# Delta rule: the 16x16 diagonal blocks of a triangular inverse on GpSimd instead of TensorE

## The chip, the cores and the metric

One core of one Trainium2 chip runs the whole kernel as one program. The metric is the device time of one execution in microseconds (us); the median of several runs counts. TensorE does the matrix products, VectorE, ScalarE and GpSimd the elementwise work, and SyncE, ScalarE and GpSimd issue the transfers (DMAs). In the rows of the profile they stand as PE (PEld is its weight load), DVE, ACT, POOL and SP.

## The reference, cut to what matters

One inference step of a decoder of two layers, for a prompt of 256 tokens and 8 samples of one token, width 2048. A layer mixes (four mLSTM heads and eight heads of the gated delta rule, from one input projection), attends to a memory of 256 tokens, and runs a SwiGLU feed-forward. The part that the change touches is the delta rule over the prompt:

```python
def step(S, xs):                                  # one chunk of the prompt
    qc, kc, vc, gc, bc = xs
    g = jnp.cumsum(gc, axis=1)
    ...
    kk = jnp.einsum('bthd,bshd->btsh', kc, kc)
    A = jnp.where(strict[None, :, :, None], decay_ts * kk * bc[:, None, :, :], 0.0)
    eg = jnp.exp(g)
    rhs = vc - eg[..., None] * jnp.einsum('bthd,bhde->bthe', kc, S)
    U = lax.linalg.triangular_solve(jnp.transpose(A, (0, 3, 1, 2)), jnp.transpose(rhs, (0, 2, 1, 3)),
                                    left_side=True, lower=True, unit_diagonal=True)
    wu = bc[..., None] * jnp.transpose(U, (0, 2, 1, 3))
    ...
```

For each head and chunk a unit triangular system (I + A) U = rhs is solved. The reference cuts the prompt into chunks of 64 tokens; the kernel takes two chunks of 128 and computes the same recurrence.

## The kernel before, in words

**Streams.** All large products are weight streams. A block of 128 x 1024 weights (512 KB) is loaded by SyncE into one of four buffers `raw`, and split exactly into two parts of float32r: `wh` by ScalarE (a copy that rounds) and `wl` by VectorE (`raw - wh`), three buffers each. TensorE then runs 24 products of 264 columns (256 tokens and 8 samples) on a block, into `acc`. Loads and splits carry a higher priority than the rest.

**Order of TensorE.** Its order is written by hand, by a small planner. A chain of small products is a generator that yields how long its next product must wait for other engines, in ns (`yield 2100.0`). `clock` adds up TensorE's own work as it is issued, by a formula (columns / 2.4 ns, four times that for float32); `pump()`, called after every few products of a stream, issues the next piece of each chain whose time on this clock has come. The planner fixes an order alone: if an input is late on the chip, TensorE waits. The order of the other engines, SyncE's queue and GpSimd's among them, comes from the scheduler's simulation, by priority and readiness; they keep that order too.

**The mixers.** Per layer, four groups of two delta-rule heads. For each group three streams (`q`, `k`, `v`) are followed by a convolution on VectorE (`y`, with a small part of it on GpSimd) and an activation (`s`). Then two chains start: `gdn_prompt` for the 256 tokens and `gdn_sample` for the samples (its products `dks` and `dS`; GpSimd makes `wm` for the latter). A group's `gdn_prompt` starts only after that of the group before has `formed` its states. GpSimd also loads states (`S`, `Ct`) and takes roots and reciprocals as powers (`kd`, `qd`, `oss`).

**gdn_prompt.** Four matrices at a time (two heads, two chunks), 128 x 128 each, side by side in tiles of 128 x 512. In order: keys transposed (`kT`); the products `kk` and `kq`; `N`, strictly upper triangular, by four VectorE operations (line 57); values and queries transposed (`vT`, `qT`). Then the inverse `Dm` of I + N and its transpose `Dt`. `Dm` starts as `ident`; a block size of 1 is doubled on VectorE alone (`u`). `N` is transposed by TensorE (`NT`) and copied to `A` by ScalarE. For b = 2, 4, 8, 16, 32, 64 a doubling step follows: four products `pp` (from `A` and `Dm`), a masked copy `Pf` on VectorE, four products `pd` (from `Dt` and `Pf`), `Dm` less `pd` on VectorE, and up to b = 16 a transposition of `Dm` to `Dt` on VectorE. Each half step is a yield (2100 ns ahead of `pp`, 1900 ns ahead of `pd`). A product in float32 shows as two matmul records in the trace. After the inverse come the two chunks (`pu`, `pS`, `pr`), and after a hold of 14200 ns the transposition `oT` of the output.

Small helpers record most operations, so that many rows carry their lines: L72 is `mm`, L76 `tr` (TensorE), L60 `tt`, L57 `stt` (VectorE, `tt` also GpSimd), L54 `copy` (ScalarE), L245 the load of `raw`, L807 and L734 the stores of delta-rule states.

Of the kernel before, what the change touches and what calls it, by code (L numbers as in the profile page):

```python
# [8 lines left out]
F32 = mybir.dt.float32  # L9
F32R = mybir.dt.float32r  # L10
AF = mybir.ActivationFunctionType
ALU = mybir.AluOpType
# [3 lines left out]
P = 128  # L16
D = 2048
KT = D // P
T = 256
# [11 lines left out]
PRIO = 1000  # L31
Q0, K0, V0, O0 = 0, 512, 1024, 2048
# [6 lines left out]
def bc(ap, axis, n):  # L39
    """ap with a new dimension of n at axis, of step 0."""  # L40
    a = ap.unsqueeze(axis)
    shape = list(a.shape)
    shape[axis] = n
    return a.to_broadcast(shape)
# [3 lines left out]
def kernel(ctx: ExitStack, tc: tile.TileContext, io: dict, outs: list):  # L48
# [14 lines left out]
    # A chain is a generator: it yields how long its next product must wait for other engines (ns). The clock counts  # L63
    # the tensor engine's work as it is issued; it only sets the order.
# [43 lines left out]
    pm = ctx.enter_context(tc.tile_pool(name="misc", bufs=4, space=PSUM))  # L108

# [10 lines left out]
    # exponents  # L120
# [4 lines left out]
    def power(t, e):  # L125
        """t ** e for e = hp, hm, in place"""
        if len(t.shape) == 3:
            e = e[:t.shape[0], :t.shape[1] * t.shape[2]].rearrange("p (a b) -> p a b", a=t.shape[1])
        else:
            e = e[:t.shape[0], :t.shape[1]]  # L130
        tt(t, t, e, ALU.pow, pool)

    # shf: out[m] = in[m - 32] - in[m] for m >= 32, on 64 partitions
# [6 lines left out]
    # for block size b: up[p, j] = 1 where row p is in the first half of pair j of blocks  # L140
    up = {}
    b = 1
# [10 lines left out]
    # twos[p, r] = 1 at p = 64 + r and 96 + r for r < 8, and at p = r - 8 and 24 + r for the others  # L153
# [4 lines left out]
    # msk[p, b] = 1 where p % 32 == b; hsel[p, h] = 1 where p % 4 == h  # L158
# [33 lines left out]
    def consts():  # L192
# [3 lines left out]
        # the gains of heads stand before 1 + tanh, twice the sigmoid  # L196
# [37 lines left out]
    def split_gain(h, l, src, g):  # L234
        """the parts of src * g, g per partition"""
        copy(h, src, scale=g)
        stt(l, src, g, h.bitcast(F32), ALU.mult, ALU.subtract)
# [11 lines left out]
    def stream(src, r0, nk, f0, xs, n=2):  # L249
        """[128, C] sums over nk row tiles, for n = 2 or 4 tiles of columns from f0; xs(k) gives the two parts of x."""  # L250
# [16 lines left out]
    def add_stream(src, r0, nk, hh, hl, nx=None, n=2):  # L267
        """x += src[r0 : r0 + nk * 128]^T h; the last one hands each tile to the next norm"""
# [10 lines left out]
    class Norm:  # L279
# [36 lines left out]
        def turn(self, t0):  # L316
            """tiles from t0, time on partitions"""
# [25 lines left out]
    def scaled(o, nx, out, k=1.0):  # L343
        """out[:, j] = k * r * o[j]"""
# [33 lines left out]
    class Gates:  # L378
        """tq: see there; over the samples: gs, exp(log decay) | a on all partitions; gn, exp(log decay), beta | a, w,
        exp(-m) with the samples on partitions; over the prompt, time on partitions: gT with m at 0, c at 32, sums of  # L380
        log decay at 64, beta at 96; em = exp(-m); eg and en = +-exp(sum of log decay) in the second chunk"""

    def gates(l, o, nx, mx, G, rstd):
# [8 lines left out]
        with tc.high_priority(offset=PRIO):  # L392
# [7 lines left out]
            # ln(1 + e) = ln(u) + (e - (u - 1)) / u with u = 1 + e as it rounds  # L400
# [7 lines left out]
            # log forget gate, its sums over time  # L408
# [11 lines left out]
            # log decay of the delta rule, its sums over each chunk  # L420
# [9 lines left out]
            # beta  # L430
# [4 lines left out]
            # c = i - b, M = max(m0, running max of c), m = b + M  # L435
        yield 20000.0
        with tc.high_priority(offset=PRIO):
# [15 lines left out]
            # the rows to spread over all partitions, in two parts: log decay sums at 64 and 96, M at 32 and 0  # L453
# [43 lines left out]
    def spread(out, G, r):  # L497
        """row r of tq's sums of parts on every partition: log decay sums of head r, or M of head r - 8"""
        mm(out, bc(twos[:, r], 1, P), G.tq)

# [1 line left out]
    def three(dst, src, swap):  # L502
        """the parts of src on 8 partitions at rows 0, 32 and 64: h, h, l, or with swap h, l, h"""
# [5 lines left out]
    def rank1(S, k3, r3, decay, mx, w):  # L509
        """S[b] = decay[b] * S[b] + k[b] r[b]^T, for states [128, 8, w]"""  # L510
# [11 lines left out]
    # Products of the samples' queries with their matrix memories, in float32r: block b of kqz, 40 b + 32 on, holds the  # L522
    # parts of sample b's query at b and 64 + b. Blocks overlap; rows that other samples' columns reach are not read.
    def columns(kqz, j, src):
        """the two parts of src, [128, 8]"""
# [4 lines left out]
    def state_parts(S, M):  # L530
        """the two parts of states, [128, 512]"""
# [5 lines left out]
    class Mix:  # L537
        """tiles of the mixers' pool"""
# [9 lines left out]
        def n(self, name, shape=(2, P)):  # L548
            """samples on partitions"""
# [24 lines left out]
    def gdn_decay(g, G, M, R):  # L574
        """E[s, i, t] = exp(sum of log decays over (s, t]), 0 for t < s; eL = exp(sum over the second chunk)"""
# [16 lines left out]

    def gdn_prompt(l, g, s, G, M, R):
# [11 lines left out]
        # keys with time on partitions; 4 (sum of squares + eps)  # L605
# [13 lines left out]
        # products of keys and queries, [s, t]  # L619
# [24 lines left out]
        # Dm = (I + N)^-1 and its transpose, by doubling the size of the diagonal blocks  # L644
        Dm, Dt, A = M.w("Dm"), M.w("Dt"), M.w("A")
        pool.tensor_copy(out=Dm, in_=bc(ident, 1, 4))
        u = M.v("u", (4, 64))
        tt(u, N[:, :, 1::2], bc(up[1], 1, 4), ALU.mult)
        tt(Dm[:, :, 1::2], Dm[:, :, 1::2], u, ALU.subtract)
# [6 lines left out]
        b = 2  # L656
        while b < P:
# [3 lines left out]
            # from 32 on a pair's products stand alone: rows r of the first half, rows r + b of the second  # L661
# [32 lines left out]
        # two chunks  # L694
# [61 lines left out]
    def gdn_sample(l, g, s, G, M, R, S, smp):  # L756
        """one step, 16 columns (head, sample); block b of kqf holds sample b's key at b and its query at 32 + b"""
# [67 lines left out]
    def twice_silu(out, y):  # L825
        """out = (1 + tanh(y / 2)) y"""
# [32 lines left out]
    def mlstm_decay(h, G, M, R):  # L859
        """d[s, t] = exp(c[s] - M[t]), 0 for t < s: the first chunk's s over both chunks' t, the second's over its own"""  # L860
# [74 lines left out]
    def mlstm_sample(l, g, q, k, vs, G, M, R, Cs, smp):  # L935
# [54 lines left out]
        # states and normalisers  # L990
# [62 lines left out]
    def conv_state(l, M, cb, st):  # L1053
        # the convolution's old rows, channels on partitions
# [19 lines left out]
    def conv_out(l, M, rawc):  # L1074
        """the convolution's new rows"""
# [91 lines left out]
    class Memory:  # L1167
        """the memory's tiles with channels on partitions, in two parts, and its rows' 1 / rms"""
# [41 lines left out]
        def times(self, src, make):  # L1210
            """two [128 tokens, 512] sums of mem @ src; make: the tiles are made on the way"""
# [20 lines left out]
    def cross_sample_scores(g, ap, qT, kc, sel, qn, scr):  # L1232
        """scores of heads 2g and 2g + 1, as products along the free axis, the memory tokens on partitions"""
# [21 lines left out]
    def cross_sample(l, ap, scr, parts, oh, ol):  # L1255
        sc = 128 ** -0.5
        # block b of pz, 64 columns: the parts of the samples' weights at 4 b and 32 + 4 b
# [36 lines left out]
        # of the products with all heads' values each row keeps its own head's  # L1294
# [234 lines left out]
```

## Time and profile before

| | |
|---|---|
| runs, us | 3010.35, 3010.87, 3012.55; median 3010.87 |
| span of the profiled execution, first to last instruction | 3007.7 us; its own time outside the span is not listed apart; the median lies 3.2 us above the span |
| granted TensorE clock over the span | 0.994 |
| busy share: TensorE, weight load, VectorE, ScalarE, GpSimd | 98%, 95%, 67%, 47%, 21% |
| DMA | 530 MB, 176 GB/s; SyncE's queue busy for 54% of 16 engines' time |
| delta rule over the prompt runs | about 87 to 413 us (first layer) and 1567 to 1890 us (second) |

How to read it: a row of a timeline has start (us), duration (us), engine, line, operation, what it writes and reads (out<-in), shapes, and in brackets the idle time ahead of it with what ended it. A row of a tile has durations in ns as least/median/greatest. A row of groups has count, busy us, mean ns, and idle time ahead. Matmuls overlap in the pipeline, so their cost is read from one start to the next and not from their durations.

### The profile page before, as it was taken

To read this page: it belongs to the slowest core of one execution; us is meant where nothing else is said; L and a number is where in the kernel's file an instruction comes from. 1 tells how busy PE (TensorE), PEld (TensorE's weight loads), DVE (VectorE), ACT (ScalarE), POOL (GpSimd) and SP (SyncE) were. 2 spreads that over 40 slices of the span, in tenths; PEclk is the share of its full clock that TensorE was granted. 3 is DMA by queue.
4 is the path that set the end of the run, shared out by engine and by line. 5 is a ranking of instruction groups with operands and counts; after the bars stand their busy time and mean duration, and the time that the engine had idled before them with its cause. 6 is when DMAs were issued, how large, how long until landed. Compare 5 with 4: busy or idle time off the path is not lost. (4 is left out here: it accounts for less than half of the span.)

```text
span 3007.7 us, 57999 instructions
## 1 busy us (share of the span) xinstructions
PE 2939.8 (98%) x23475; PEld 2862.8 (95%) x23475; DVE 2027.1 (67%) x3333; ACT 1405.6 (47%) x2249; POOL 624.5 (21%) x756
## 2 busy tenths in 40 slices
PE   8999999999999999999999999999999999999998
PEld 7999999978999999999999999999799999999998
DVE  7888786878555555555688877778775555555555
ACT  6545444466434333333464444445654333334335
POOL 5323232354100000000143332124520000000101
PEclk9999999999999999999999999999999999999999
DMA  7544555666555555555655553746755555555554
GB/s 195 143 143 151 152 184 163 216 209 193 182 179 181 182 179 180 182 182 179 182 156 150 159 161 125 223 147 212 223 180 180 181 183 180 180 181 182 178 181 134
DMA packets 381251, 530.09 MB, mean 176 GB/s; under 512 B 25576, under 2 KB 226224, under 8 KB 380960
## 3 DMA queue, kind: packets, MB, share of 16 engines
q1 hardware_dynamic: 363584, 498.47, 53.9%
q0 software_dynamic: 7424, 25.20, 2.7%
q10 hardware_dynamic: 9976, 2.72, 0.5%
q8 instruction: 184, 3.01, 0.4%
q14 instruction: 83, 0.68, 0.1%
HBM read 502.88 MB, written 23.83 MB: 175 GB/s over the span
## 5 line engine op out<-in xcount | busy, mean ns | idle before, releaser
L60 DVE TENSOR_TENSOR wl<-raw,wh 128x1024 fp32r<-128x1024 f32 x880 | 1096.7, 1247 | 796.7 <-ACT wh L54 794.7
L54 ACT ACTIVATE wh<-raw 128x1024 fp32r<-128x1024 f32 x880 | 931.5, 1059 | 1299.0 <-PE acc L72 1196.2
L72 PE MATMUL acc<-xh,wh 128*128 128x264 f32 x4736 | 1370.9, 289 | 6.5 <-ACT wh L54 4.3
L72 PE MATMUL acc<-xl,wh 128*128 128x264 f32 x4736 | 1351.1, 285 | 1.6 <-DVE xl L57 1.6
L72 PE MATMUL acc<-xh,wl 128*128 128x264 f32 x4736 | 1351.9, 285 | 0.5 <-DVE wl L60 0.5
L72 PEld LDWEIGHTS acc<-xh,wh 128*128 128x128 f32 x4736 | 897.7, 190 | 11.4 <-ACT wh L54 4.4
L72 PEld LDWEIGHTS acc<-xl,wh 128*128 128x128 f32 x4736 | 898.7, 190 | 4.9 <-DVE xl L57 2.3
L72 PEld LDWEIGHTS acc<-xh,wl 128*128 128x128 f32 x4736 | 897.1, 189 | 1.2 <-DVE wl L60 1.1
L72 PE MATMUL acc<-ffh,wh 128*128 128x264 f32 x1408 | 401.0, 285 | 0.6 <-DVE xT L60 0.5
L72 PE MATMUL acc<-ffl,wh 128*128 128x264 f32 x1408 | 401.0, 285 | 0.0
L72 PE MATMUL acc<-ffh,wl 128*128 128x264 f32 x1408 | 400.5, 284 | 0.0
L60 POOL TENSOR_TENSOR fg<-fg,rstd 128x264 f32<-128x264 f32 x88 | 95.5, 1117 | 1305.9 <-ACT fg L1411 1305.9
L72 PEld LDWEIGHTS acc<-ffh,wh 128*128 128x128 f32 x1408 | 265.0, 188 | 1.0 <-issue 1.0
L72 PEld LDWEIGHTS acc<-ffl,wh 128*128 128x128 f32 x1408 | 265.4, 188 | 0.0
L72 PEld LDWEIGHTS acc<-ffh,wl 128*128 128x128 f32 x1408 | 265.1, 188 | 0.0
L60 DVE TENSOR_TENSOR xT<-acc,xT 128x264 f32<-128x264 f32 x512 | 190.6, 425 | 21.4 <-PE acc L72 21.1
L60 POOL TENSOR_TENSOR sa<-sa,sq 128x264 f32<-128x264 f32 x96 | 92.4, 980 | 179.1 <-ACT sq L313 178.8
L60 POOL TENSOR_TENSOR wm<-r,msk 72x512 fp32r<-72x512 f32 x64 | 78.7, 1238 | 166.5 <-PE dS L72 124.1
L57 DVE SCALAR_TENSOR_TENSOR xl<-xT,cst,xh 128x264 fp32r<-128x264 f32 x96 | 77.1, 838 | 0.9 <-ACT xh L54 0.7
L57 DVE SCALAR_TENSOR_TENSOR y<-y,cst,y 128x255 f32<-128x255 f32 (+1 forms) x144 | 65.3, 491 | 0.9 <-ACT y L54 0.4
L60 POOL TENSOR_TENSOR sl<-Ct,sh 128x512 fp32r<-128x512 f32 x32 | 48.9, 1536 | 72.6 <-ACT sh L54 47.4
L54 ACT ACTIVATE xh<-xT,cst 128x264 fp32r<-128x264 f32 x80 | 39.6, 507 | 28.5 <-DVE xT L60 28.5
(510 smaller groups left out, 3436.3 us busy)
## 6 DMA issues: line engine op xcount, KB each, us to landing
raw<-in_w_in_dram SPq DMA_DIRECT2D x224, 512.0 KB
raw<-in_ffn_w_gate_dram SPq DMA_DIRECT2D x176, 512.0 KB
raw<-in_ffn_w_up_dram SPq DMA_DIRECT2D x176, 512.0 KB
raw<-in_ffn_w_down_dram SPq DMA_DIRECT2D x176, 512.0 KB
raw<-in_w_out_dram SPq DMA_DIRECT2D x64, 512.0 KB
S<-in_state_gdn_S_dram POOLq DMA_DIRECT2D x16, 512.0 KB, 6.4
out_dram<-S SPq DMA_DIRECT2D x16, 512.0 KB
Ct<-in_state_mlstm_C_dram POOLq DMA_DIRECT2D x8, 1024.0 KB, 8.1
```

Source lines behind the costliest of these rows:

```text
L54: act.activation(out, in_, AF.Copy, scale=scale)
L57: dve.scalar_tensor_tensor(out=out, in0=a, scalar=s, in1=b, op0=o0, op1=o1)
L60: (eng or dve).tensor_tensor(out=out, in0=a, in1=b, op=op)
L72: pe.matmul(out=out, lhsT=lhsT, rhs=rhs, start=start, stop=stop)
```

## The change

The steps b = 1, 2, 4 and 8 of the doubling go. In their place `base_blocks` inverts the 16 x 16 diagonal blocks of I + N by Gauss steps on GpSimd: the four matrices of a group have eight such blocks each, and each of the 32 blocks is put on a partition of its own. As blocks lie on different partitions of `N`, they go through DRAM: SyncE stores `N` (256 KB, to an area whose row pitch lets one access pattern reach all blocks), gathers the blocks (`Nb`, runs of 64 bytes), GpSimd does 15 steps of two operations each on all blocks at once (a product into `tb`, a subtraction from `Db`), SyncE stores the result and gathers it back with rows on partitions (`Dc`, 128 x 4 x 16), and GpSimd spreads it into the block diagonal of `Dm` with the mask `own`. `Nb` and `Db` lie in the tile of `Dt`. TensorE's doubling begins at b = 16; ahead of it the planner gets a further hold of 12500 ns after the transposition of `N`. Comments are removed as well, without effect.

```diff
+BASE = 16
...
+    turn = ctx.enter_context(tc.tile_pool(name="turn", bufs=2, space=bass.MemoryType.DRAM))
...
     up = {}
-    b = 1
+    b = BASE
     while b < P:
...
+    own = cp.tile([P, P // BASE], F32, name="own")      # 1 where partition p lies in block j
...
+    def base_blocks(N, Dm, room, M):
+        nb, e = P // BASE, BASE * BASE
+        step = BASE * P + BASE
+        nd = turn.tile([4 * nb * step], F32, name="nd")
+        dd = turn.tile([4 * nb * e], F32, name="dd")
+        nc.sync.dma_start(out=bass.AP(nd.tensor, nd.offset, [[P, P], [nb * step, 4], [1, P]]), in_=N)
+        Nb, Db = (room[:4 * nb, i * e:(i + 1) * e].rearrange("p (r c) -> p r c", c=BASE) for i in range(2))
+        tmp = M.c("tb", (e // 4,))[:4 * nb]
+        nc.sync.dma_start(out=Nb, in_=bass.AP(nd.tensor, nd.offset, [[step, 4 * nb], [P, BASE], [1, BASE]]))
+        pool.memset(Db, 0.0)
+        pool.memset(Db.rearrange("p r c -> p (r c)")[:, ::BASE + 1], 1.0)
+        for k in range(BASE - 1):
+            w = BASE - 1 - k
+            t = tmp[:, :(k + 1) * w].rearrange("p (r c) -> p r c", c=w)
+            d = Db[:, :k + 1, k + 1:]
+            tt(t, Db[:, :k + 1, k:k + 1].to_broadcast([4 * nb, k + 1, w]),
+               Nb[:, k:k + 1, k + 1:].to_broadcast([4 * nb, k + 1, w]), ALU.mult, pool)
+            tt(d, d, t, ALU.subtract, pool)
+        nc.sync.dma_start(out=dd.rearrange("(p e) -> p e", e=e), in_=Db.rearrange("p r c -> p (r c)"))
+        Dc = M.c("Dc", (4, BASE))
+        nc.sync.dma_start(out=Dc, in_=bass.AP(dd.tensor, dd.offset, [[BASE, P], [nb * e, 4], [1, BASE]]))
+        tt(Dm.rearrange("p i (n c) -> p i n c", c=BASE), bc(Dc, 2, nb), bc(bc(own, 1, 4), 3, BASE), ALU.mult, pool)
...
         Dm, Dt, A = M.w("Dm"), M.w("Dt"), M.w("A")
-        pool.tensor_copy(out=Dm, in_=bc(ident, 1, 4))
-        u = M.v("u", (4, 64))
-        tt(u, N[:, :, 1::2], bc(up[1], 1, 4), ALU.mult)
-        tt(Dm[:, :, 1::2], Dm[:, :, 1::2], u, ALU.subtract)
+        base_blocks(N, Dm, Dt.rearrange("p i t -> p (i t)"), M)
         dve.transpose(Dt.rearrange("p i t -> p (i t)"), Dm.rearrange("p i t -> p (i t)"))
         yield 2700.0
         pa = ps("NT")
...
         copy(A, four(pa))
-        b = 2
+        yield 12500.0
+        b = BASE
         while b < P:
```

More of the change, by code (lines that the diff above doesn't have):

```diff
@@ L152 @@
         b *= 2
+    own = cp.tile([P, P // BASE], F32, name="own")
+    dve.memset(own, 1.0)
+    pool.affine_select(out=own, in_=own, pattern=[[-BASE, P // BASE]], compare_op=ALU.is_ge, fill=0.0, base=0,
+                       channel_multiplier=1)
+    pool.affine_select(out=own, in_=own, pattern=[[BASE, P // BASE]], compare_op=ALU.is_ge, fill=0.0, base=BASE - 1,
+                       channel_multiplier=-1)
     twos = cp.tile([P, GH + MH], F32R, name="twos")
@@ L378 @@
     class Gates:
+        pass
     def gates(l, o, nx, mx, G, rstd):
```

## The prediction

> **What bounds the kernel now.** I read the page's busy times first, then the window over the second layer's chains of the delta rule (busy us of each engine, granted clock).
>
> ```profile
> span 3007.7 us, 57999 instructions
> PE 2939.8 (98%) x23475; PEld 2862.8 (95%) x23475; DVE 2027.1 (67%) x3333; ACT 1405.6 (47%) x2249; POOL 624.5 (21%) x756
> core 0: us, PE busy (x) PEld busy (x) DVE busy (x) ACT busy (x) POOL busy (x), PEclk, DMA share, GB/s
> 1566.00:1866.00 300.00, 293.20 (x2484) 284.95 (x2483) 242.64 (x541) 143.15 (x329) 89.14 (x128) 0.99 0.49 149
> ```
>
> Then TensorE's timeline around a doubling step (start, us, what, in brackets a wait ahead of it):
>
> ```profile
> 111.87 1.54 PE L72 MATMUL pp<-Dm,A 128*128 128x64 f32 x8 [2.35 <-DVE Dm L60]
> ...
> 113.74 0.42 PE L72 MATMUL acc<-xh,wh 128*128 128x264 f32 x1
> 113.96 0.42 PE L72 MATMUL acc<-xl,wh 128*128 128x264 f32 x1
> ...
> 116.69 0.28 PE L72 MATMUL acc<-xh,wl 128*128 128x264 f32 x1
> 116.81 1.00 PE L72 MATMUL pd<-Pf,Dt 128*128 128x64 f32 x8
> 117.62 0.47 PE L72 MATMUL dS<-wm,k 72*128 72x512 f32 x1
> 1589.49 0.77 PE L72 MATMUL pd<-Pf,Dt 128*128 128x64 f32 x5 [1.71 <-DVE Pf L60]
> 512.39 0.59 PE L72 MATMUL acc<-gd2h,wh 128*128 128x264 f32 x1 [3.25 <-DVE xT L60]
> ```
>
> and the window behind the wait of 512.39, columns as above:
>
> ```profile
> 511.70:518.50 6.80, 6.11 (x28) 6.11 (x29) 6.37 (x14) 3.47 (x8) 4.17 (x3) 0.50 0.25 80
> ```
>
> TensorE has next to no gaps where the chains run: between the delta rule's links the planner issues weight-stream products. So a product taken off TensorE is worth its whole time, and a wait put in front of TensorE costs its whole time, as TensorE keeps the written order. The start-to-start times price a doubling product: `pd` starts at 116.81, the next instruction at 117.62, so four f32 products (eight records) cost 0.81 us. The rows also price a wait beyond its length: after 2.35 us of idling the stream's products start every 0.22 us (113.74, 113.96) instead of 0.12 (116.69, 116.81), and after 3.25 us the granted clock stands at 0.50 for 6.8 us. Half of the half-speed time is lost: about 1.5 us after the short wait, 3.1 us after the long one.
>
> **What goes.** Of six doubling steps (b = 2 to 64) three go in each of eight chains (four groups, two layers): 2 products x 3 steps x 8 = 48, at 0.81 us = 38.9 us. Two waits ahead of such products go too, 2.35 and 1.71 us (rows above), with a clock loss of about 1.5 us each: 7 us. **Gain: 46 us.** VectorE loses work as well (its groups by shape, window from 100 to 402 us, the first layer's four chains; count, busy us and mean ns):
>
> ```profile
> L60 DVE TENSOR_TENSOR wl<-raw,wh 128x1024 fp32r<-128x1024 f32 x66 | 81.4, 1234 | 16.0 <-ACT wh L54 15.5
> L690 DVE STREAM_TRANSPOSE Dt<-Dm 128x512 f32<-128x512 f32 x16 | 11.3, 706 | 0.2
> L60 DVE TENSOR_TENSOR Dm<-Dm,pd 128x256 f32<-128x256 f32 x16 | 6.7, 417 | 9.5 <-PE pd L72 9.2
> ```
>
> `Dm` and `Dt` alone are 0.42 + 0.71 us a step, 3.4 us a chain; VectorE, busy for 242.6 of 300 us against TensorE's 293.2, is not the bound, so I count nothing. The copy of `ident` on GpSimd and the step b = 1 go; two memsets come in, done while GpSimd waits for the gather; the masks are built at the start. Nothing for any of these.
>
> **What comes, and its cover.** Between N and the first remaining product, one serial chain: store N, gather the blocks, 30 GpSimd operations, store, gather, one spreading multiply. Hidden is what lies behind the 12.5 us (and 2.1 us) for which the planner holds the chain back, in its own clock, plus the lead of N over `NT`. From that point TensorE waits.
>
> ```profile
> 104.74 1.13 DVE L57 SCALAR_TENSOR_TENSOR N<-kk,bs,E 128x128 f32<-128x128 f32 x4
> 106.49 0.60 PE L76 MATMUL NT<-ident,N 128*128 128x128 f32 x4
> 248.26 0.61 PE L72 MATMUL pS<-wu,kw 128*128 128x128 f32 x4
> 265.51 0.60 PE L76 MATMUL oT<-ident,o 128*128 128x128 f32 x4
> 1644.20 0.68 PE L72 MATMUL pS<-wu,kw 128*128 128x128 f32 x4
> 1662.51 0.60 PE L76 MATMUL oT<-ident,o 128*128 128x128 f32 x4
> 1571.86 1.13 DVE L57 SCALAR_TENSOR_TENSOR N<-kk,bs,E 128x128 f32<-128x128 f32 x4
> 1581.17 0.60 PE L76 MATMUL NT<-ident,N 128*128 128x128 f32 x4
> ```
>
> N is complete 0.6 us ahead of `NT` in the first chain (104.74 + 1.13 to 106.49) and 8.2 in the fifth (1571.86 + 1.13 to 1581.17); these are the ends of eight chains, whose mean is 4.9. How long is 14.6 us of the planner's clock? It holds the chain 14.2 us between `pS` and `oT`; that takes 17.3 and 18.3 us from start to start, of which about 0.9 are the products: 14.2 become 16.4 to 17.4, a factor of 1.18 or so. Then 14.6 become 17.3, with `NT` itself and the rounding of a second hold 18. **Cover: 4.9 + 18 = 23 us on average, 18.6 in the first chain.**
>
> The GpSimd steps first:
>
> ```profile
> L60 POOL TENSOR_TENSOR cb<-bT,cst x2: 588/590/592, 44.6 to 1526.1; 128x192 f32<-128x192 f32 x2
> L60 POOL TENSOR_TENSOR y<-y,cb x48: 193/429/1237, 51.0 to 1757.3; 128x8 f32<-128x8 f32 x48
> 48.54 1.66 POOL L60 TENSOR_TENSOR tmpc<-bT,cst 128x192 f32<-128x192 f32 x1
> 50.28 0.59 POOL L60 TENSOR_TENSOR cb<-cb,tmpc 128x192 f32<-128x192 f32 x1
> 48.55 1.23 DVE L60 TENSOR_TENSOR wl<-raw,wh 128x1024 fp32r<-128x1024 f32 x1 [0.20 <-ACT wh L54]
> L60 POOL TENSOR_TENSOR wm<-r,msk x64: 1029/1038/2329, 103.3 to 2048.4; 72x512 fp32r<-72x512 f32 x64
> L57 DVE SCALAR_TENSOR_TENSOR y<-y,cst,y 128x255 f32<-128x255 f32 (+1 forms) x144 | 65.3, 491 | 0.9 <-ACT y L54 0.4
> ```
>
> Undisturbed, 192 elements take 588 ns and 8 take 193: 0.176 us + 2.15 ns an element. The two operations of step k have (k+1)(15-k) elements, 680 over the 15 steps, so 30 x 0.176 + 1360 x 2.15 ns = 8.2 us. Each needs the one before it; such a pair (48.54 + 1.66 to 50.28) has 0.08 us between: 30 x 0.08 = 2.4. That is 10.6 us alone. But the `tmpc` of 48.54 took 1.66 us where its like take 0.59: VectorE's `wl`, which reads two SBUF operands, began at 48.55 and held it off. `wl` fills 81.4 of 302 us; the convolution's `y`, of two SBUF operands too, 65.3 of the some 600 us that the chains last in both layers: 27% + 11% of the time. If every blocked moment added, 10.6 / 0.62 = 17 us; as dispatch and the 0.08 us run on under a wait, less: I take 14 (10.6 to 17). One more us (0 to 3) for other GpSimd work that falls between.
>
> Now the transfers:
>
> ```profile
> nN<-in_state_mlstm_n_dram POOLq DMA_DIRECT2D x4, 8.0 KB, 1.8
> kc<-in_cache_mem_k_dram POOLq DMA_DIRECT2D x32, 256.0 KB, 5.3
> 1468.45 0.40 ACTq L357 DMA_DIRECT2D graw<-in_w_in_dram  x1
> q10 hardware_dynamic: 4164, 0.20, 39.4%
> 122.68 0.35 DVE L57 SCALAR_TENSOR_TENSOR S<-S,gs,dS 128x128 f32<-128x128 f32 x1
> 123.05 0.38 SPq L807 DMA_DIRECT2D out_dram<-S  x1
> ```
>
> The smallest lands in 1.8 us, 256 KB in 5.3. A gather of 2048 pieces of 64 bytes, issued at 1468.45, was through by the end of the window from 1466 to 1472.6, whose 4164 packets are it and its sister: within 4.1 us. SyncE issues a store the moment its data is done (122.68 + 0.35, then 123.05): it stands waiting. The 32 blocks are 512 pieces of 64 bytes. I take 3.5 us for N (256 KB; 1.8 to 5.3), 2.7 for the 512 pieces (1.8 to 4.1), 2.0 for 32 KB back (1.8 to 4.1), 2.7 for 512 pieces again (1.8 to 4.1): 10.9, all nearer the small rows because SyncE, waiting, has no weight load in front of them. The spreading multiply, 512 elements with broadcasts as `wm`, 1.6 us (1.0 to 2.3); hand-overs 0.5.
>
> **Sum.** 10.9 + 14 + 1 + 1.6 + 0.5 = 28.0 us from N, against 23 of cover: a wait of 5 us in each chain, 40 us in all, and after each the half clock, 2.3 us between the two prices above: 18. Loss 58, gain 46, net +12: span 3007.7 to about 3020. The median of the runs lies 3.2 us above this span: **3023 us**, 0.4% slower. Every us by which the chain is longer or shorter is worth 8; it breaks even at 26.5 us.
>
> The Trainium skill, DMA: Bandwidth & Descriptors, section Anatomy of one DMA — SWDGE (gpsimd) path, gives 2 us plus bytes at 436 GB/s a transfer (measured there for queues written by GpSimd); by it the four would come to an estimated 9 us, not 10.9, and the chain to 26. The 256 KB row (5.3 us, not 2.6) disagrees; no row here shows the others.
>
> **SyncE's queue.** Four transfers stand in it among the weight loads. The second and fourth wait for the landing of the one ahead, the third for GpSimd; weight loads behind them stand still for perhaps 3, 5 and 2 us. Four raw buffers at 302 / 66 = 4.6 us a block are 18 us of reserve less the load's own 5 us: covered, and if not it falls mostly into the time in which TensorE waits anyway. On GpSimd the samples' `wm` and the `y` of the next stream queue behind the 30 steps; TensorE waits for both later, inside the same wait. The chains lose six half steps (`pp` to `pd`, 111.87 to 116.81, is one of the longest) and gain the wait: they end at about the same time, and each is waited for only after later streams, so I count nothing after the mixers.
>
> **Rivals.** (1) The cover holds: GpSimd near its undisturbed 10.6 us and transfers near 2 us make 10.6 + 8 + 2 = 21 us, under 23. Then all of the 46 us is gained: 2965; at 24.5 us, with short waits and some half clock, about 2990. For it: those are prices seen in rows. Against: `wl` alone takes 27% of the time, and the first chain has only 18.6 us of cover. It decides below 26.5 us. (2) Wait and saving cancel, the chain at 26 to 27 us, as with transfers 2 us shorter than I take in all, still above four times 1.8: 3005 to 3017. The skill's transfer prices lead here too. (3) Weight loads held up longer than the reserve, or GpSimd stuck in its order behind an operation that waits for VectorE (`y` on VectorE running late), 4 us more a chain: 3060. For it: GpSimd's queue holds such waits now. Against: TensorE idles at that time anyway. (4) The change doesn't shorten TensorE's work, since VectorE is the bound: VectorE stands at 81% in the window and TensorE at 98%, so I give it nothing.
>
> **How the numbers follow.** Forecast (waits of 4.5 to 8 us a chain; 3017 to 3045) 0.42; rival 1 0.32; rival 2 0.14; rival 3 0.12. A change under 0.2% (6 us) can't be told from none. Faster 0.32, same 0.14, slower 0.54. The range runs from 2972 (the cover holds but for the first chain, and some clock loss) to 3072 (a chain of 33 us, its transfers and steps towards their upper ends: 8 x 10.3 + 8 x 3.1 - 46 = +61): both signs are in it, and the forecast's own range is 3017 to 3045.
>
> **What would show it.** Right: eight gaps of TensorE before the first `pp` of a chain, ended by GpSimd's `Dm`, 4 to 8 us (the first about 9), with the granted clock at 0.5 behind them; `pp` and `pd` down from 448 records to 256 each; 30 small GpSimd operations in about 14 us. Wrong: no such gaps (rival 1), or gaps at weight-stream products that wait for ScalarE's `wh` and a late load (rival 3).

## The result, and the profile after

The changed kernel takes 3049.99 us (median of 4 runs, 3049.26 to 3051.84) against 3011.71 us (3010.35 to 3013.78) for the kernel before in the same comparison: a ratio of 1.0136 on record, 95% interval 1.0124 to 1.0148 (these two medians by themselves give 1.0127). It is slower, as forecast, but by 1.3% and not by 0.4%: 27 us more than the 3023 us predicted, inside the range (2972 to 3072) and above the forecast's own one (3017 to 3045).

The page after, its span and its line of busy times, and then the window over the second layer's chains. In the changed kernel the helpers' lines stand one lower than before (L73 for `mm`, L77 `tr`, L61 `tt`, L58 `stt`, L55 `copy`). The columns of the window are busy us of PE, PEld, DVE, ACT and POOL, granted clock, DMA share and GB/s:

```profile
span 3047.2 us, 57440 instructions
PE 2912.1 (96%) x23091; PEld 2832.1 (93%) x23091; DVE 1988.6 (65%) x3242; ACT 1404.1 (46%) x2249; POOL 726.5 (24%) x1006
```

```profile
1566.00:1866.00 300.00, 264.17 (x2152) 256.24 (x2151) 214.61 (x471) 137.50 (x322) 138.15 (x253) 0.94 0.52 149
```

TensorE has 27.7 us less work by the page and yet ends 39.5 us later. In the window it was busy for 293.20 us at a clock of 0.99; now it is 264.17 at 0.94. VectorE's busy time fell with it, from 242.64 to 214.61 us. It has less work there (471 instructions for 541), and it waits too, as its rows below show.

TensorE's waits before at the same places (what waited, for whom; us in total, times, longest):

```profile
PE acc L72 <- ACT wh L54: 4.3, 1, 4.3
...
PE pp L72 <- DVE Dm L60: 3.5, 3, 2.4
...
PE dks L76 <- POOL kv L761: 0.2, 1, 0.2
```

and after:

```profile
PE pp L73 <- POOL Dm L61: 48.2, 5, 15.1
...
PE mC L73 <- DVE mkw L61: 9.9, 1, 9.9
PE dks L77 <- POOL kv L794: 6.9, 2, 6.6
...
PE dks L77 <- POOL mvn L928: 4.8, 1, 4.8
PE dS L73 <- POOL wm L61: 4.0, 2, 3.2
PE acc L73 <- ACT wh L55: 3.4, 1, 3.4
```

and the first of the three kinds in its timeline:

```profile
138.93 1.97 PE L73 MATMUL pp<-Dm,A 128*128 128x64 f32 x8 [15.11 <-POOL Dm L61]
...
218.53 0.69 PE L77 MATMUL dks<-ident,kv 128*128 128x128 f32 x2 [6.62 <-POOL kv L794]
...
370.19 2.08 PE L73 MATMUL mC<-mvn,mkw 128*128 128x257 f32 x4 [9.90 <-DVE mkw L61]
```

Five of the eight chains show the forecast wait at `pp`. The others wait as well, but elsewhere: at the samples' `dks` in the second and third chain, at the mLSTM's `mC` in the fourth. The one wait for `wh` comes at the start of the kernel, before as after: where the chains run, no weight block was late. Why is to be seen on GpSimd and VectorE. GpSimd in the first two chains:

```profile
113.43 0.20 POOL L61 TENSOR_TENSOR tb<-Dt 32x15 f32<-32x15 f32 x1
...
114.30 2.16 POOL L61 TENSOR_TENSOR Dt<-Dt,tb 32x28 f32<-32x28 f32 x1
116.42 1.03 POOL L61 TENSOR_TENSOR wm<-r,msk 72x512 fp32r<-72x512 f32 x1
...
131.65 0.22 POOL L61 TENSOR_TENSOR Dt<-Dt,tb 32x15 f32<-32x15 f32 x1
...
137.83 1.05 POOL L61 TENSOR_TENSOR Dm<-Dc,own 128x512 f32<-128x512 f32 x1 [3.65 <-DMA Dc<-dd]
138.82 0.19 POOL L794 COPY kv<-s 128x16 f32<-128x16 f32 x1
...
217.29 1.05 POOL L61 TENSOR_TENSOR Dm<-Dc,own 128x512 f32<-128x512 f32 x1 [3.52 <-DMA Dc<-dd]
218.28 0.20 POOL L794 COPY kv<-s 128x16 f32<-128x16 f32 x1
```

The steps last from 113.43 to 131.87, 18.4 us. One of them took 2.16 us where its forerunner of the same size took 0.22, and a `wm` stands between two steps. At 217.29 GpSimd has stood for 3.5 us at `Dm`, whose gather is under way; the samples' copy into `kv`, 0.2 us long, stands behind it, and TensorE's `dks` of 218.53 behind that copy. In the third chain the copy stands between the last step and `Dm`; the small memset `mvn` comes right behind it, and the profile puts the wait down to that. VectorE in the first and the fourth chain:

```profile
113.33 1.10 DVE L58 SCALAR_TENSOR_TENSOR S<-S,gs,dS 128x128 f32<-128x128 f32 x4
114.36 0.47 DVE L58 SCALAR_TENSOR_TENSOR y<-y,cst,y 128x253 f32<-128x253 f32 x1
114.76 1.21 DVE L61 TENSOR_TENSOR wl<-raw,wh 128x1024 fp32r<-128x1024 f32 x1
115.89 0.46 DVE L58 SCALAR_TENSOR_TENSOR y<-y,cst,y 128x253 f32<-128x253 f32 x1
...
354.83 0.55 DVE L61 TENSOR_TENSOR mW<-mqk,d 128x384 f32<-128x384 f32 x1
368.33 0.71 DVE L682 STREAM_TRANSPOSE Dt<-Dm 128x512 f32<-128x512 f32 x1 [12.95 <-POOL Dm L61]
368.96 0.84 DVE L58 SCALAR_TENSOR_TENSOR gd2l<-ox,cst,gd2h 128x256 fp32r<-128x256 f32 x2
369.72 0.42 DVE L61 TENSOR_TENSOR mkw<-mkT,d 128x256 f32<-128x256 f32 x1
```

Above: the step of 114.30 ended at 116.46, after `y`, `wl` and again `y`, three operations of VectorE with two SBUF operands, had run one behind the other, the last until 116.36. Below: VectorE stood for 12.95 us at the first transposition of `Dm`, and `mkw`, which depends on no Gauss step, was late for TensorE by 9.9 us.

**The balance.** By the trace's records of the granted clock, TensorE was busy at half clock for 26.0 us before and 57.2 us after; I count half of that as lost. Its work at full clock thus went from 2926.8 to 2883.5 us, its idle time (span less busy) from 67.9 to 135.1: -43.3 of work, +15.6 of half clock, +67.2 of idling, together the 39.5 us by which the span grew.

### The profile page after: what moved, and what is told of

Its sections match the earlier page's. It is cut to its first block, busy times and chain, and to the rows that moved or that the text cites. A ratio compares the mean times of both kernels' runs of the same rounds, so it can differ in the third digit from the quotient of the medians.

```text
span 3047.2 us, 57440 instructions
## 1 busy us (share of the span) xinstructions
PE 2912.1 (96%) x23091; PEld 2832.1 (93%) x23091; DVE 1988.6 (65%) x3242; ACT 1404.1 (46%) x2249; POOL 726.5 (24%) x1006
## 4 chain that ended last, share of the span: by engine, by line
PE 76%; DVE 9%; POOL 5%; DMA 4%; ACT 3%; issue 3%; ACTq 0%; SPq 0%; POOLq 0%; DVEq 0%
PE acc L73 68%; DVE wl L61 3%; POOL Dt L61 2%; PE kv L73 2%; POOL tb L61 2%; DVE xl L58 1%; ACT wh L55 1%; PE dks L73 1%; DMA nd<-N 1%; DMA Dc<-dd 1%; DMA Dt<-nd 1%; DVE xT L61 0%; PE pp L73 0%; PE accg L73 0%; DVE y L58 0%
## 5 line engine op out<-in xcount | busy, mean ns | idle before, releaser
L61 DVE TENSOR_TENSOR wl<-raw,wh 128x1024 fp32r<-128x1024 f32 x880 | 1100.0, 1251 | 805.7 <-ACT wh L55 804.1
L55 ACT ACTIVATE wh<-raw 128x1024 fp32r<-128x1024 f32 x880 | 931.2, 1059 | 1309.1 <-PE acc L73 1191.6
L73 PE MATMUL acc<-xh,wh 128*128 128x264 f32 x4736 | 1370.4, 289 | 5.7 <-ACT wh L55 3.4
L73 PE MATMUL acc<-xl,wh 128*128 128x264 f32 x4736 | 1352.9, 286 | 1.7 <-DVE xl L58 1.7
L73 PE MATMUL acc<-xh,wl 128*128 128x264 f32 x4736 | 1353.2, 286 | 1.0 <-DVE wl L61 0.8
L73 PEld LDWEIGHTS acc<-xh,wh 128*128 128x128 f32 x4736 | 899.9, 190 | 10.9 <-issue 3.8
L73 PEld LDWEIGHTS acc<-xl,wh 128*128 128x128 f32 x4736 | 900.6, 190 | 4.9 <-DVE xl L58 2.3
L73 PEld LDWEIGHTS acc<-xh,wl 128*128 128x128 f32 x4736 | 898.9, 190 | 2.2 <-DVE wl L61 2.1
L61 POOL TENSOR_TENSOR fg<-fg,rstd 128x264 f32<-128x264 f32 x88 | 95.3, 1112 | 1306.0 <-ACT fg L1444 1286.4
L73 PE MATMUL acc<-ffh,wh 128*128 128x264 f32 x1408 | 400.9, 285 | 0.6 <-DVE xT L61 0.5
L73 PE MATMUL acc<-ffl,wh 128*128 128x264 f32 x1408 | 401.0, 285 | 0.0
L73 PE MATMUL acc<-ffh,wl 128*128 128x264 f32 x1408 | 400.5, 284 | 0.0
L73 PEld LDWEIGHTS acc<-ffh,wh 128*128 128x128 f32 x1408 | 264.9, 188 | 1.0 <-issue 0.9
L73 PEld LDWEIGHTS acc<-ffl,wh 128*128 128x128 f32 x1408 | 265.4, 188 | 0.0
L73 PEld LDWEIGHTS acc<-ffh,wl 128*128 128x128 f32 x1408 | 265.0, 188 | 0.0
L61 DVE TENSOR_TENSOR xT<-acc,xT 128x264 f32<-128x264 f32 x512 | 190.2, 423 | 19.6 <-PE acc L73 19.6
L61 POOL TENSOR_TENSOR sa<-sa,sq 128x264 f32<-128x264 f32 x96 | 93.9, 995 | 178.9 <-ACT sq L322 178.6
L61 POOL TENSOR_TENSOR wm<-r,msk 72x512 fp32r<-72x512 f32 x64 | 79.5, 1250 | 152.6 <-PE dS L73 112.1
L58 DVE SCALAR_TENSOR_TENSOR xl<-xT,cst,xh 128x264 fp32r<-128x264 f32 x96 | 76.4, 831 | 0.7 <-ACT xh L55 0.7
L73 PE MATMUL pp<-Dm,A 32*32 32x32 f32 (+2 forms) x256 | 21.8, 245 | 48.7 <-POOL Dm L61 48.2
L73 PEld LDWEIGHTS pp<-Dm,A 32*32 32x32 f32 (+2 forms) x256 | 18.8, 156 | 52.6 <-POOL Dm L61 49.2
L58 DVE SCALAR_TENSOR_TENSOR y<-y,cst,y 128x255 f32<-128x255 f32 (+1 forms) x144 | 65.8, 492 | 0.4
```

What stands on the lines that cost most here:

```text
L55: act.activation(out, in_, AF.Copy, scale=scale)
L58: dve.scalar_tensor_tensor(out=out, in0=a, scalar=s, in1=b, op0=o0, op1=o1)
L61: (eng or dve).tensor_tensor(out=out, in0=a, in1=b, op=op)
L73: pe.matmul(out=out, lhsT=lhsT, rhs=rhs, start=start, stop=stop)
```

## The experiments

Twelve kernels, each timed against the kernel before. Theory A: TensorE waits for a chain longer than its cover, and, as its second part, for other work that stands behind the chain in another engine's order. Rivals: SyncE's queue (B), VectorE's standing at the transposition (C), and those named with each run. "Full-clock work", "half clock lost" and "idle" are TensorE's, in us, from each kernel's profiled run as in the balance above. Each ratio is to runs of the kernel before in the same comparison, whose medians lay between 3007.7 and 3011.7. The profiled run of e9 was 9 us faster than its median, those of e3 and e5 4 and 5 us slower, and their last three columns are to be read so.

| kernel | median us | ratio to before (95%) | full-clock work | half clock lost | idle |
|---|---|---|---|---|---|
| before | 3011.7 | | 2926.8 | 13.0 | 67.9 |
| after | 3050.0 | 1.0136 (1.0124, 1.0148) | 2883.5 | 28.6 | 135.1 |
| e1 steps left out | 2966.9 | 0.9857 (0.9840, 0.9873) | 2884.1 | 12.1 | 70.2 |
| e2 transposition written later | 3048.5 | 1.0129 (1.0114, 1.0144) | 2884.8 | 28.9 | 133.0 |
| e3 kv on ScalarE | 3040.5 | 1.0103 (1.0088, 1.0118) | 2886.2 | 26.3 | 129.8 |
| e4 steps on VectorE | 3045.9 | 1.0122 (1.0107, 1.0137) | 2883.1 | 32.4 | 130.4 |
| e5 blocks of 8 | 3047.5 | 1.0125 (1.0107, 1.0142) | 2899.2 | 31.4 | 119.8 |
| e6 steps beside the doubling | 3037.2 | 1.0093 (1.0074, 1.0111) | 2927.6 | 25.7 | 79.4 |
| e7 way back by GpSimd | 3066.6 | 1.0191 (1.0176, 1.0206) | 2884.0 | 29.7 | 149.9 |
| e8 longer hold | 3035.3 | 1.0088 (1.0073, 1.0104) | 2886.5 | 29.9 | 117.9 |
| e9 longer hold, kv on ScalarE | 3026.5 | 1.0055 (1.0038, 1.0072) | 2885.7 | 24.9 | 105.5 |
| e10 and GpSimd cleared | 3025.0 | 1.0058 (1.0041, 1.0074) | 2884.6 | 26.0 | 111.7 |
| e11 before, cleared likewise | 3007.8 | 1.0004 (0.9993, 1.0015) | 2926.4 | 11.3 | 68.7 |
| e12 no transposition on VectorE | 3019.4 | 1.0034 (1.0021, 1.0046) | 2884.2 | 30.0 | 104.0 |

**e1, the steps left out.**

```
-        for k in range(BASE - 1):
-            ...
-            tt(t, Db[:, :k + 1, k:k + 1]..., Nb[:, k:k + 1, k + 1:]..., ALU.mult, pool)
-            tt(d, d, t, ALU.subtract, pool)
```

> Leaves the 30 GpSimd operations of the Gauss steps out; the four transfers, the two memsets and the spreading multiply stay, so the diagonal blocks come out as identities. Theory A (the time is lost because the serial chain from N to Dm is longer than its cover, mostly by the steps, which took 10.9 to 23.4 us of 31.0): the chain falls to about 13 us, under the cover of every group; the waits at pp, at the samples' products and at mC go, 67 us of TensorE idling and some 15 us of half clock with them: about 2965. Rival B (the transfers and SyncE's queue hold the weight loads up): waits stay in most groups, 3010 to 3040.

2966.9 us. The page, then the window over the second layer's chains:

```profile
span 2966.3 us, 57184 instructions
PE 2896.1 (98%) x23091; PEld 2818.2 (95%) x23091; DVE 1987.0 (67%) x3242; ACT 1404.7 (47%) x2249; POOL 646.7 (22%) x766
```

```profile
1566.00:1866.00 300.00, 291.33 (x2456) 282.85 (x2455) 241.62 (x511) 148.20 (x318) 107.23 (x133) 0.99 0.57 164
```

No wait for GpSimd's `Dm` at `pp` and none at `mC` is left; one of 5.8 us at `dks` is, in the first chain. The whole gain of the shorter doubling is there, 42.7 us of full-clock work. The edit takes away more than the operations: with nothing to invert, the transfers back no longer wait for those there, and `Dm` was ready 6.7 to 12.7 us after N rather than 13. So it shows what the chain costs in all, and that the transfers, all four issued by SyncE, do not slow TensorE when nobody waits in between. B is out in the form in which the transfers themselves cost. The form in which SyncE's standing holds weight loads up is answered by the changed kernel's own waits: the only one for `wh` is that at the start.

**e2, the transposition written later.**

```
-        dve.transpose(Dt..., Dm...)
         yield 2700.0
         ...
         yield 12500.0
+        dve.transpose(Dt..., Dm...)
```

> The first transposition of Dm is written behind the hold of 12.5 us instead of ahead of it, so VectorE doesn't stand at it with other work behind. Theory A (TensorE waits for GpSimd's Dm itself in most groups): only the wait at mC (9.9 us, VectorE's mkw stood behind the transposition) goes, with about 3 us of half clock: 3035 to 3040. Rival C (VectorE's 59.9 us of standing at the transposition is what starves TensorE): most of the loss goes, 2985 to 3010.

3048.5 us: neither. VectorE stood as before,

```profile
DVE Dt L688 <- POOL Dm L61: 59.6, 8, 12.8
```

for 59.6 us (59.9 in the changed kernel). All 3242 of VectorE's operations come in the same order in both kernels, so the order doesn't follow from where the line stands; that it follows from when the scheduler expects `Dm` is likely, but not shown. The run tests nothing of C; e12 does.

**e3, the samples' copies on ScalarE.**

```
-            pool.tensor_copy(out=kv[:, :, at:at + NB], in_=s[kind][:, :, T:C])
+            copy(kv[:, :, at:at + NB], s[kind][:, :, T:C])
```

(`kqf` likewise.)

> The samples' copies into kv and kqf (five a group) go from GpSimd to ScalarE. Theory A with its second part (work that stands behind the steps in GpSimd's order makes TensorE wait elsewhere): the waits at dks of the second and third group (6.6 and 4.8 us) go, some 2 us of them come back as a wait at pp; with the half clock about 14 us less, 3034 to 3040. Rival D (GpSimd's order costs nothing, TensorE would wait as long at pp): 3048 to 3052.

3040.5 us, 9.5 less than the changed kernel: just outside A's figure, far from D's. The 6.6 and 4.8 us at `dks` became 2.3 and 1.1, and 1.8 us came up at `pp` of the third chain. Work behind the chain in GpSimd's order does hold TensorE up.

**e4, the steps on VectorE.** With e2's edit, and

```
-            tt(t, ..., ALU.mult, pool)
-            tt(d, d, t, ALU.subtract, pool)
+            tt(t, ..., ALU.mult)
+            tt(d, d, t, ALU.subtract)
```

> The 30 operations of the Gauss steps go from GpSimd to VectorE, with the transposition behind the hold as in the kernel that moves it alone. VectorE's operations on a few elements take 0.15 to 0.2 us each start to start (mrd rows), so 30 take some 6 us alone, and up to 14 with the weights' wl and the convolution's y between them. Theory A: the chain is 21 to 27 us against about 23 of cover: 2965 to 3000. Rival E (VectorE, busy for 81% of the time there, falls behind with the weights' low parts, and TensorE waits at the weight streams): 3030 or more.

3045.9 us: A's range is missed, and the time lies in E's, but not for E's reason. The weights' `wl` cost TensorE only 2.9 us; it waited 61.2 us at `pp`, six times. The chain was no shorter: `Dm` was ready 20 to 43 us after N. VectorE in the fifth chain:

```profile
1592.30 0.18 DVE L61 TENSOR_TENSOR tb<-Dt 32x39 f32<-32x39 f32 x1
1592.41 1.21 DVE L61 TENSOR_TENSOR wl<-raw,wh 128x1024 fp32r<-128x1024 f32 x1
...
1595.08 0.18 DVE L61 TENSOR_TENSOR Dt<-Dt,tb 32x39 f32<-32x39 f32 x1
...
1617.04 0.21 DVE L61 TENSOR_TENSOR tb<-Dt 32x64 f32<-32x64 f32 x1
1617.29 0.21 DVE L61 TENSOR_TENSOR Dt<-Dt,tb 32x64 f32<-32x64 f32 x1
```

A step takes 0.2 us and, where two come together, 0.24 from start to start: 30 in 7 us. But between two of them the order has a `wl`, a `y`, an `S`: 2.8 us from 1592.30 to 1595.08. On average the 30 operations were busy for 5.9 us and lasted 19.7: here the chain is as long as what the engine's order puts between them.

**e5, blocks of 8.**

```
-BASE = 16
+BASE = 8
-        yield 12500.0
+        yield 8300.0
```

> Blocks of 8 by Gauss steps (14 operations on 64 partitions, 168 elements in all instead of 1360) and the doubling from 8; the hold is 8.3 us of the planner's instead of 12.5, as one doubling step takes the rest. TensorE saves 32 four-product halves instead of 48: 26 us. Theory A (the chain's length against its cover decides): everything of the chain but the steps is 31.0 - 17.8 = 13.2 us, the steps 4 us alone and up to 7 with other work between, so 17 to 20 us against 4.9 + 10.4 x 1.18 + 1 = 18 of cover; waits of a few us in the first chains at most: 2985 to 2997. Rival F (what stretches the chain is the waiting of other operations in GpSimd's order, whatever the number of steps): a chain of 25 us or more, 3010 to 3030.

3047.5 us, above both expectations, with a chain between theirs. Full-clock work fell by 27.6 us (26 expected), and `Dm` was ready 17.9 to 28.4 us after N, 22.5 on average (17 to 20 expected): the 14 operations took 5.9 to 13.6 us from the first start to the last end, not 4 to 7. A step of 15 elements took 2.82 us in the sixth chain. Each chain became 8.5 us shorter, but its cover too, by some 5 us by the smaller hold (18 expected against 23), and the gain in all by 16 us; a wait at `pp` stood in six chains, the longest of 10.0 us. Fewer steps were paid for by the smaller hold and the smaller gain; as the run changes all three, it doesn't show what fewer steps alone would do.

**e6, the steps beside the old doubling.** The kernel before, and behind its copy of `ident`:

```
+        X = M.w("X")
+        base_blocks(N, X, X.rearrange("p i t -> p (i t)"), M)
```

> The kernel before, with its doubling from 2, and beside it all of the new chain (store, gather, 30 GpSimd operations, store, gather, multiply) into a tile that nobody reads. Theory A with its second part: TensorE doesn't wait for Dm, but still for work that stands behind the steps in GpSimd's order (dks 6.6 and 4.8 us, dS 3.2 us in the changed kernel), with half clock after: 15 to 25 us over the kernel before, 3025 to 3035. Rival D (only the wait for the result costs): no change, 3008 to 3014. Rival B (SyncE's standing delays the weights): gaps at weight products that wait for wh, 3030 or more.

3037.2 us, a ratio of 1.0093: nobody reads the result, and still it costs 28 us (of which 25.1 are in the profiled run: 11.5 of idle, 12.7 of half clock). TensorE's waits at `dks` rose from 0.2 to 9.6 us. A's second part is shown, D is out, and B's gaps at `wh` are not there (3.0 us, once, at the start). GpSimd in the third chain, and TensorE:

```profile
290.10 1.05 POOL L61 TENSOR_TENSOR X<-Dc,own 128x512 f32<-128x512 f32 x1 [4.21 <-DMA Dc<-dd]
291.09 0.20 POOL L798 COPY kv<-s 128x16 f32<-128x16 f32 x1
...
291.35 0.69 PE L77 MATMUL dks<-ident,kv 128*128 128x128 f32 x2 [4.40 <-POOL mvn L932]
```

GpSimd stood for 4.2 us at a multiply whose result is not wanted, and the copy that TensorE needed stood behind it (`mvn` is the memset right behind the copy).

**e7, the way back by GpSimd's queue.**

```
-        nc.sync.dma_start(out=dd..., in_=Db...)
+        nc.gpsimd.dma_start(out=dd..., in_=Db...)
```

(the gather of `Dc` likewise.)

> The store of the inverted blocks and the gather behind it are issued by GpSimd instead of SyncE, which then no longer stands for the some 18 us of the steps with weight loads behind it. Rival B (SyncE's standing costs): 10 to 30 us less than the changed kernel, 3020 to 3040. Theory A (SyncE's standing is covered by the ring of raw weights): within 8 us of 3050, with what GpSimd needs to issue transfers on top or less.

3066.6 us, 16.6 more than the changed kernel: nothing was won by freeing SyncE, as B would have it. By itself the run can't tell a small gain from GpSimd's added cost, but with no late `wh` in the changed kernel there was none to win. A's 8 us were too few. GpSimd now issues two transfers a chain (0.61 and 0.77 us in the first), and the waits grew in every place: `dks` from 11.7 to 18.4 us in all, `mC` from 9.9 to 11.4, `pp` from 48.2 to 53.2.

**e8, a longer hold.**

```
-        yield 12500.0
+        yield 16000.0 if g < 3 else 12500.0
```

> The hold behind NT is 16 us of the planner's instead of 12.5 in the first three groups of each layer, 4.1 us by the factor of 1.18; the fourth group's stays. Theory A (every us of cover is a us off each wait at pp): the waits of groups 1, 5, 6 and 7 in time (15.1, 5.0, 10.3, 8.5 us) shrink by 4.1 each, 16 us in all, with up to 4 us of half clock; the waits at dks and mC stay: 3029 to 3034. Rival C (VectorE stands at the transposition of Dm, so what TensorE gets in between runs out and the wait is found at another product): 3045 to 3050.

3035.3 us, near A's 3029 to 3034 and far from C's. But not in A's way:

```profile
PE dks L77 <- POOL kv L794: 18.1, 3, 12.9
PE dks L77 <- POOL mvn L928: 12.7, 2, 7.9
...
PE pp L73 <- POOL Dm L61: 8.0, 2, 6.9
```

At `pp` 48.2 us became 8.0, more than the 16 expected; at `dks` 11.7 became 30.8. With `pp` later, the samples' products come ahead of it, and meet the copies that stand behind the steps and `Dm` on GpSimd. Holds longer than this were not tried.

**e9, e10, e11, e12: towards a kernel that wins.** e9 has e8's and e3's edits. e10 adds

```
-                pool.tensor_copy(out=rawc[:, :, ti], in_=y0[:, j, T - 3:C])
+                copy(rawc[:, :, ti], y0[:, j, T - 3:C])
-                tt(y[:, j, T:C], y[:, j, T:C], cb[:, ti], ALU.add, pool)
+                tt(y[:, j, T:C], y[:, j, T:C], cb[:, ti], ALU.add)
```

e11 has e3's and e10's moves in the kernel before. e12 is e10 with `Dt` made on GpSimd:

```
-        dve.transpose(Dt..., Dm...)
+        pool.tensor_copy(out=Nb, in_=Db.rearrange("p r c -> p c r"))
         ... one store and one gather for both, Dc of (8, BASE) ...
+        tt(Dt..., Dc[:, 0:4]..., own..., ALU.mult, pool)
```

> Both edits at once: the hold of 16 us in the first three groups, and the samples' copies into kv and kqf on ScalarE. Theory A with its second part (the longer hold moved the waits from pp, 48.2 to 8.0 us, to dks, 11.7 to 30.8 us, since the copies into kv stand behind the steps): the 30.8 us at dks go; by the times at which Dm was ready with the longer hold, 6.6 us of them come back at pp (6.3 in the first group, 0.3 in the second); with 7 us of half clock 31 us less than the longer hold alone: 3000 to 3008. Rival C (TensorE is short of other work, so that the waits find another product): 3020 to 3035.

> As the kernel with both edits, and of the convolution the copies into rawc go from GpSimd to ScalarE and the additions y<-y,cb from GpSimd to VectorE, so that next to nothing but wm stands between the Gauss steps. Theory A2 (the steps take 17.8 us instead of the 10.9 of the fourth group because operations between them wait in GpSimd's order for VectorE and ScalarE): the steps take 11 to 13 us, the chain 25, waits only in the first group: 2980 to 2995. Rival I (VectorE's wl and y hold each step off, whatever stands between): steps of 15 us or more, 2998 to 3008.

> The kernel before with the same moves off GpSimd (kv, kqf and rawc to ScalarE, y<-y,cb to VectorE) and no Gauss steps: the comparison for the kernel with GpSimd cleared. Theory A and its rivals agree: the moves alone are worth little, 3000 to 3015.

> As the kernel with GpSimd cleared, and the first transposition of Dm leaves VectorE: GpSimd copies the inverted blocks transposed beside the others (one operation of 256 elements), the one store and the one gather behind it carry both (1024 pieces), and a second spreading multiply on GpSimd makes Dt. Theory C2 (what is left at dks, 17.9 us by way of ScalarE's kv and VectorE's s, at wh 6.3, at mC 7.2 and at pd 2.9 stands behind VectorE's transposition, which waits for Dm 5.8 to 10.4 us at a time): these go but for some 4 us that come back at pp, some 30 us, and half clock from 84.7 to 55 us, 15 us more; GpSimd's two operations add 2 us to a chain that has the room: 2978 to 2992. Rival J (VectorE then stands at the next operation that hangs on Dm, Pf, and the same work behind it): 3012 to 3028.

e11: 3007.8 us, no change, as expected. e9: 3026.5 us, C's side: of the 30.8 us at `dks` 13.8 stayed, by way of ScalarE. e10: 3025.0 us, above both its ranges and not to be told from e9; the steps took 16.4 us on average, not 11 to 13, so A2 is wrong. I's reason holds: in the second, third and seventh chain next to nothing of GpSimd's stood between the steps, and they still took 14.8 to 15.5 us. A second wait at `wh` in e10 (6.3 us) is not SyncE's: ScalarE stood for 11.7 us at an operation on the mLSTM's `hn`, with the `wh` behind it. Four rows of e10 tell where the wait at `dks` now comes from, from VectorE through ScalarE to TensorE:

```profile
134.47 0.71 DVE L682 STREAM_TRANSPOSE Dt<-Dm 128x512 f32<-128x512 f32 x1 [7.03 <-POOL Dm L61]
...
136.22 0.70 DVE L58 SCALAR_TENSOR_TENSOR s<-s,y 128x528 f32<-128x528 f32 x1
...
136.95 0.21 ACT L55 ACTIVATE kv<-s 128x16 f32<-128x16 f32 x1 [8.76 <-DVE s L58]
...
137.22 0.69 PE L77 MATMUL dks<-ident,kv 128*128 128x128 f32 x2 [10.33 <-ACT kv L55]
```

The copies left GpSimd, but their source `s` stands behind VectorE's transposition of `Dm`. e12 takes that transposition away: 3019.4 us, J's side of the two. TensorE's longest wait and VectorE's in e12, and two rows of VectorE's timeline:

```profile
PE pp L73 <- POOL Dm L61: 25.8, 6, 8.1
DVE Pf L61 <- PE pp L73: 29.7, 5, 10.8
```

```profile
140.29 0.42 DVE L61 TENSOR_TENSOR Pf<-pp,up 128x256 f32<-128x256 f32 x1 [10.81 <-PE pp L73]
...
359.51 0.69 DVE L61 TENSOR_TENSOR hn<-hn,mss 128x512 f32<-128x512 f32 x1 [8.80 <-POOL mss L61]
```

VectorE stands at the next operation that hangs on the chain, or at one whose input GpSimd has behind the steps (`mss`). And TensorE is back at `pp`: the 7.8 us that it waited there in e10 became 25.8, where C2 had some 4 in mind. The waits at `dks` and `mC` went (17.9 to 4.3 us, and 7.2 to none), so TensorE came to `pp` earlier, and the chain was 30.4 us long, 2.8 more than in e10. So the first part of A is what is left. No version tried that keeps the steps beats the kernel before; the best, e12, is 0.34% slower (0.21 to 0.46%). Whether an order of all engines made for the chain's real length would take the loss away was not tried.

## Why the prediction was right in direction and short in size

- **The gain** was predicted at 38.9 us of products and 7 us of waits and their clock. Full-clock work fell by 43.3 us, by 42.7 in e1, and the records of `pp` and `pd` from 448 to 256 each, as predicted. TensorE's waits for VectorE at `pp` and `pd` fell from 8.9 to 1.8 us, where 4.1 had been counted. Right, within 5 us.
- **The cover** was predicted at 23 us on average and 18.6 in the first chain. TensorE came to the first `pp` 18.2 us after N there (33.3 less the wait of 15.1), and 24.6 us on average over the eight chains, waits on the way taken off. Right.
- **The chain** was predicted at 28.0 us and took 31.0 on average (23.1 to 37.5). Two terms were too small: "14 us" for the 30 operations, and above all "one more us (0 to 3)" for other work between them. The operations took 13.3 us and the pauses between two that follow each other directly 1.9, so 15.1. Of the 13.3 us, 7.7 are the shortest times of these shapes and 5.6 come on top, nearly all in steps that VectorE held off: the price by row was a little high, the price of VectorE's two-operand operations too low. The other work took 3.2 us on average and 9.2 in the fifth chain, where four `wm` and several `rawc`, `qd` and `y` fell in. Together 18.4 us, not 15. The fourth chain, with only a copy of 0.2 us between, took 11.2.
- **The transfers** were predicted at 10.9 us. SyncE's rows of the first chain:

```profile
105.64 0.37 SPq L610 DMA_DIRECT2D nd<-N  x1
108.93 0.34 SPq L613 DMA_DIRECT2D Dt<-nd  x1
...
131.89 0.33 SPq L623 DMA_DIRECT2D dd<-Dt  x1
...
133.39 0.36 SPq L625 DMA_DIRECT2D Dc<-dd  x1
```

  Store to gather 3.3 us here and 3.6 on average (3.5 predicted), gather to the first step 3.2 (2.7), store back to gather 1.5 (2.0), that gather to the multiply 3.2 (2.7): 11.5. The multiply took 1.1, not 1.6. By the fit in the Trainium skill, DMA: Bandwidth & Descriptors, section Anatomy of one DMA — SWDGE (gpsimd) path, it would have been an estimated 9 us: the traces side with the rows of this case.
- **The law of 8 us for each us of chain** would give, with the 3 us that were missing, 3023 + 24 = 3047. That the measured 3050 lies near is luck, since the cover was longer too: chain by chain, the real chains and covers make TensorE wait 53 us at `pp` where 40 were predicted, and 3023 + 13 = 3036. Its idle time rose by 67.2 us, where the sum had 36 (the 40 less the 4 of waits that go). Work and half clock came within 5 us of the sum, so the idling is all of the 27 us that were missing: 13 by the chains' own lengths, and the rest, some 18, in waits elsewhere. The sentence that failed: `wm` and `y` queue behind the steps, and "TensorE waits for both later, inside the same wait". In the second, third and fourth chain the waits were 6.6, 4.8 and 9.9 us at `dks` and `mC`, where `pp` by itself lacked 0.3, 1.6 and nothing. Not seen at all: `kv` behind the steps or `Dm` on GpSimd, and VectorE's transposition, at which it stood for 59.9 us with other work behind. e3 and e6 show the first by itself; for the second there are the rows of the fourth chain and of e10. So of the signs that would have shown the forecast right, "eight gaps before the first `pp`" came as five, the first of 15.1 us instead of about 9.
- **Half clock** was predicted at 18 us, with some 3 saved at the waits that go; it cost 15.6 more. The size is right, but partly by luck: it was reckoned for eight waits of 5 us at `pp`, and paid for fewer and longer ones there and others elsewhere.
- **SyncE's queue** was counted at nothing: right. No product waited for `wh` where the chains run, and e7 won nothing.
- **Rival 1** (the cover holds) gave 2965 us, and e1, where the chain is short, took 2966.9: the price was right and the condition was not met. **Rival 3** came nearer in time than the forecast's middle, 3060 us by a chain 4 us longer (3 in fact), with a chance of 0.12, but not by its causes: no weight load was late, and GpSimd was not stuck among the steps waiting for VectorE's results. It was running other work there, and VectorE's two-operand operations held it off.

## What to carry to other kernels

Work moved off a full engine onto an idle one brings its order with it: what stands behind the new chain on that engine, and behind an operation that consumes the chain's result on any other, comes late with it, even where the chain's own result is in time or nearly so, as in the second to fourth chain here. So price such a move in two parts: the chain against its cover, and the chain beside the old work with its result unread (e6), which alone cost 28 us here against a gain of 43. And a short dependent chain isn't 30 times its shortest row, but 30 places in an order with neighbours on its own engine (3.2 us here) and on VectorE (5.6 us here).

## What the runs showed of the hardware that was not expected

- An operation of GpSimd can be held off by more than one operation of VectorE in a row: the step of 114.30 took 2.16 us, through `y`, `wl` and `y`, where the same shape takes 0.22 to 0.23 undisturbed, and one step of the sixth chain took 3.30. Over the eight chains 75 of the 240 operations took over 0.06 us longer than the shortest of their shape, and 74 of these ended 0.06 to 0.17 us after a `wl`, `y` or `s` of VectorE. The three operations ahead of 114.30 ran wholly under VectorE's `S` of 113.33, whose `dS` lies in PSUM, and took their usual 0.20 to 0.22 us. The Trainium skill, SBUF — State Buffer, section SBUF: two separate sides, says that an operation of VectorE with two SBUF inputs that starts first keeps GpSimd out for its whole length; the trace agrees, and shows that the next ones may take the turn too (the record of the step of 114.30 begins 0.07 us ahead of that of `y`, so it doesn't show which came first).
- Small waits cost as much again in clock: in e6 TensorE idled 11.5 us more than before and lost 12.7 us more at half clock. In the changed kernel, with longer waits, 67.2 us of idling cost 15.6.
- Steps of 15 to 64 elements take 0.20 to 0.31 us on GpSimd in the fourth chain, but for one that was held off, and 0.15 to 0.22 on VectorE (e4, but for one of 1.04): for operations this small the engines differ little, and the neighbours decide.
